# Packing the fetched choices of 32 tokens into full tiles

## The chip, the core and the metric

The kernel runs on one core of one Trainium2 chip. The metric is the device time of one execution in microseconds. Three runs before the change took 2815.97, 2822.40 and 2823.87 us, a median of 2822.4. The engines are TensorE (PE), VectorE (DVE), ScalarE (ACT), GpSimd (POOL) and SyncE (SP), which issues most DMAs; POOL issues the indirect ones. Each engine takes its instructions in the order of its own queue.

## The reference

Two transformer layers run over 256 tokens of 2048 features. The change lies in the second half of the first layer, a product-key mixture of experts with 16,384 experts and 128 choices for each token (8 heads, 16 each):

```
idx, g = top-k over pairs of sub-keys          # 256 tokens x 128 choices
a = einsum('cd,ced->ce', xc, expert_u[ic])     # one dot product per choice
w = g * gelu(a)
y = einsum('ce,ced->cd', w, expert_v[ic])      # weighted sum of 128 rows of v
```

An expert's number is 128 times its first key plus its second. The attention before and the second layer behind are not touched.

## The kernel before

All activations against u are computed densely: 128 streams of two 512 KB loads each, every load split into a high and a low fp32r part (h by ACT, l by DVE, `hi_lo`), then 24 matmuls with 256 columns on PE. Three raw buffers and three split buffers let SP, ACT and DVE run ahead of PE.

For v the experts are parted by their second key. Those from 72 (`PICKED`) on, 56 of 128, are done densely: `build` and `apply` scatter the gates into `grid`, and `dense_rows` streams v twice (two halves of the columns, d = 0 and 1), 56 steps each. Those below 72 are fetched: for every token an indirect DMA on POOL reads up to 128 rows of 8 KB of `v_rows` (`fetch_row`), those of the other sort being out of bounds and left out; another reads the 128 activations (`fetch_act`) from `picked`, a DRAM copy of the gelu outputs. `weigh` multiplies them by the gates into a window of zeros, and four matmuls of 128x32 on 128x512 add the token's row to a bank that holds 32 tokens by 2048 columns.

`choose` finds the choices in the background of the u streams (i from 0 to 52): top-k on DVE, one-hots on POOL and DVE, then for each half of the tokens three transposes of keys and gates on PE, and from them `slots`, `gate`, `at_row` and `at_act`. From i = 75 on, `unit` is called once for every u load and every dense step; at `PACE` 1.27 tokens a call it runs three tokens (`LOT`) at a time. `FETCH` 6 row buffers are in flight, values are fetched 20 tokens ahead (`AHEAD`) and weighed eight at a time (`SOON`). Finished banks are stored to `y_rows` (SP) and read back by POOL (`add_y`), which DVE adds to h. The fetches, the products and the top-k carry order tokens; everything else is ordered by a scheduler by readiness, so the queues differ from the program's order.

Of the kernel before, what the change touches and what calls it, by code (L numbers as in the profile page):

```python
# [26 lines left out]
T = 256  # L27
NM = 16
TM = T + NM
PICKED = 72  # L30
GRID = 128 - PICKED

# [12 lines left out]
def _constants():  # L45
    i = np.arange(128)
    ident = np.eye(128)
    iota = np.broadcast_to(i[None, :], (128, 128))
    base = np.concatenate([ident, iota, np.ones((128, 128))], 1)
    tri = np.where(i[None, :] <= i[:, None], 0.0, NEG)  # L50
    anti = np.where(i[None, :] > i[:, None], 0.0, NEG)
    causal = np.concatenate([tri, np.zeros((128, 128)), tri], 1)
    inv = 10000.0 ** (-(np.arange(32, dtype=np.float32)) / np.float32(32.0))
    inv = np.broadcast_to(inv.astype(np.float32)[None], (128, 32))
    lo = np.tile(_t5_thresholds(), 4)[:, None]
    front = np.concatenate([causal, anti, inv, lo], 1)
# [3 lines left out]
    return [np.ascontiguousarray(a.astype(np.float32)) for a in (base, front, back)]  # L60

# [22 lines left out]


def _layout(a):
    base, front, back = _constants()
    x = a["x"][0]  # L90
    L = {"c_base": base, "c_front": front, "c_back": back}
    L["x"] = x.reshape(2, 128, D)
    L["xT"] = x.T.reshape(KD, 128, T).transpose(1, 0, 2)
    pos = a["positions"][0]
# [207 lines left out]
def bc(ap, shape):  # L302
    return ap.to_broadcast(shape)
# [14 lines left out]
def chain(*gens):  # L318
    for g in gens:
        yield from g  # L320
# [571 lines left out]
def experts(S, I, x2, r2, started, keep, bst, grid, alloc_xn, close_x2, close_xn, late, picked, y_rows):  # L892
# [34 lines left out]
    sc_ = carve(2, 16, 128)  # L927
    keysT = carve(16, 128)
    bcr = carve(T)
    spare = [carve(T) for _ in range(4)]  # L930
    S.load(keysT, I["keysT"])

    def renorm(k):

# [36 lines left out]
    gate = rp.tile([128, T], F32, name="gate")  # L971
    at_row = rp.tile([128, T], U32, name="at_row")
    at_act = rp.tile([128, T], U32, name="at_act")
    got = rp.tile([128, T], F32, name="got")
    fetched = [rp.tile([128, D], F32, name=f"fetched{i}") for i in range(FETCH)]

    windows = [rp.tile([128, 33, 32], F32, name=f"window{i}") for i in range(2)]

    def choose():
        iota16 = S.iota[:, 0:16]  # L980
        for t in range(2):
# [41 lines left out]
            ve.tensor_copy(gate[:, ts], ps[:, 256:384])  # L1023

            x, y = eqs[0].rearrange("p a b -> p (a b)")[:, :128], eqs[1].rearrange("p a b -> p (a b)")[:, :128]
            po.tensor_scalar(x, slots[:, 1, ts], PICKED - 0.5, 128.0 * PICKED, ALU.is_ge, ALU.mult)
            po.tensor_tensor(x, x, slots[:, 1, ts], op=ALU.add)
            ve.scalar_tensor_tensor(x, slots[:, 0, ts], float(PICKED), x, ALU.mult, ALU.add)
            ve.tensor_copy(at_row[:, ts], x)
            ve.scalar_tensor_tensor(y, x, float(T), S.iota, ALU.mult, ALU.add)  # L1030
            if t:
                po.tensor_scalar(y, y, 128.0, None, ALU.add)
            ve.tensor_copy(at_act[:, ts], y)
            yield

    made = {}
# [31 lines left out]

    acts = picked.rearrange("i j (t o) -> (i j t) o", o=1)

    def fetch(*args, **kw):
        tc.stamp_issue_order_token(po.indirect_dma_start(*args, **kw).ins, 'po')  # L1072

    def fetch_act(t):
        fetch(got[:, t:t + 1], None, acts, bass.IndirectOffsetOnAxis(at_act[:, t:t + 1], 0),
                              bounds_check=128 * PICKED * T - 1, oob_is_err=False)

    def fetch_row(t):
        fetch(fetched[t % FETCH], None, I["v_rows"], bass.IndirectOffsetOnAxis(at_row[:, t:t + 1], 0),
                              bounds_check=128 * PICKED - 1, oob_is_err=False)  # L1080

    def weigh(t0):

        ve.tensor_tensor(windows[t0 // 32 % 2][:, t0 % 32:t0 % 32 + 8, 31], got[:, t0:t0 + 8], gate[:, t0:t0 + 8], op=ALU.mult)

    def picks():

        for t in range(AHEAD):
            fetch_act(t)
        for t in range(0, SOON, 8):  # L1090
            weigh(t)
        yield
        stages = []
        for t in range(T):
            g, tt = t // 32, t % 32
            if tt == 0:
                out = S.bank()
            w = windows[g % 2].rearrange("p a b -> p (a b)")[:, 32 * tt + 31 - tt:32 * tt + 63 - tt]
            r = fetched[t % FETCH]
            for c in range(4):  # L1100
                S.mm(out[32 * c:32 * c + 32], w, r[:, 512 * c:512 * c + 512], start=tt == 0, stop=tt == 31)
            if t + FETCH < T:
                fetch_row(t + FETCH)
            if t + AHEAD < T:
                fetch_act(t + AHEAD)
            if t % 8 == 2 and t + SOON < T + 2:
                weigh(t + SOON - 2)
            if tt == 31:
                stage = rw.tile([128, 512], F32, tag="stage", name=S.name("stage"))
                act.copy(stage, out)  # L1110
                stages.append((t + 2, g, stage))
            if stages and (t >= stages[0][0] or t == T - 1):
                _, g_, stage = stages.pop(0)
                for c in range(4):
                    S.load(y_rows[32 * g_:32 * g_ + 32, 512 * c:512 * c + 512], stage[32 * c:32 * c + 32])
            yield
# [16 lines left out]
    for i in range(128):  # L1133
        S.pe_token = 'pe' if i >= PICKED else None
        for a in S.stationary_steps(I["u"], 2 * i, 2, 8, 128, xn, slice(0, T)):
            if i >= PICKED + LEADP:
                unit()
        if i < PICKED:
            if i % 4 == 0:
                lot = rw.tile([128, 4, T], F32, tag="lot", name=S.name("lot"))  # L1140
            act.activation(lot[:, i % 4], a, AF.Gelu_apprx_tanh)
            if i % 4 == 1 and pending:
                S.load(*pending.pop())
            if i % 4 == 3:
# [12 lines left out]
        due += CR  # L1157
        if due >= 1.0:
            next(bg, None)
            due -= 1.0  # L1160
        if i == FIRST - 2:
            for _ in bg:
                pass
            S.token = None
            for f in fetched + windows + [got]:
                po.memset(f, 0.0)
            for t in range(FETCH):
                fetch_row(t)
            build(0)
            ahead = 4  # L1170
        while ahead and gated < T and gated < (i + 2 - FIRST) * RATE:
            if ahead < T:
                build(ahead)
                ahead += 4
            apply(gated, max(i + 1 - PICKED, 0))
            gated += 4
    while gated < T:
        if ahead < T:
            build(ahead)
            ahead += 4  # L1180
        apply(gated, GRID)
        gated += 4
    ob.close()
    close_xn()

# [8 lines left out]
    def add_y(t, c):  # L1194
# [3 lines left out]
        ve.tensor_tensor(h[:, t, cs], h[:, t, cs], y, op=ALU.add)  # L1198

    for d, i in dense_rows(S, wp, I["v"], GRID, lambda i: grid[:, i], evac):  # L1200
# [12 lines left out]
    return h  # L1213
# [457 lines left out]
```

## Time and profile before

| | |
|---|---|
| median of three runs | 2822.4 us |
| profiled execution | 2810.0 us |
| its span, first to last instruction | 2808.2 us |
| PE busy | 2741.8 us (98%) |
| DVE, ACT, POOL busy | 1604.4, 1337.8, 724.4 us |
| granted clock of PE, mean | 0.993 |

Busy time of PE is a union: matmuls overlap in it, so the step from one to the next is read from their starts. A group's mean is the duration of one instruction; a DVE or POOL row's bracket gives the idle time before it and what ended it. The DMA share is the mean busy share of the core's 16 DMA engines.

### The profile page before, as it was taken

The page shows a single profiled execution, that of the slowest core. Times are in us where ns is not written, and L with a number is a line of the kernel's source. Part 1 is how long each engine was busy: PE and PEld are TensorE (multiplying, and loading weights), DVE is VectorE, ACT ScalarE, POOL GpSimd, SP SyncE. Part 2 cuts the span into 40 slices and gives each one's busy share as a digit, 9 for nine tenths or more (in the row PEclk, how much of TensorE's full clock was granted, in tenths as well). Part 3 has the DMA queues.
Part 4 walks back from the last instruction along what each step waited for, and adds up shares of the span by engine and source line. Part 5 has one row for each costly group of instructions (what it writes and reads, how often), then busy time and mean ns, then how long its engine had stood idle before and what let it go on. Part 6 is the DMA issues. An engine that isn't in the chain of part 4 may idle for free.

```text
span 2808.2 us, 48986 instructions
## 1 busy us (share of the span) xinstructions
PE 2741.8 (98%) x19080; PEld 2325.8 (83%) x19080; DVE 1604.4 (57%) x2652; ACT 1337.8 (48%) x2306; POOL 724.4 (26%) x675
## 2 busy tenths in 40 slices
PE   7999999999998999999999999999999999999998
PEld 5977999999996777777566666898789999988886
DVE  5867788677664555543344445654654444466665
ACT  5654544444553444432333334543445555555554
POOL 1200003202016666665767761102000000000000
PEclk9999999999999999999999999999999999999999
DMA  6533656766666888898989997544656666666665
GB/s 209 152 131 114 209 173 199 262 218 222 205 189 214 289 299 301 293 323 297 323 321 340 343 323 246 165 155 125 188 180 194 195 193 193 194 194 195 188 194 165
DMA packets 177064, 625.81 MB, mean 223 GB/s; under 512 B 41321, under 2 KB 42217, under 8 KB 156665
## 3 DMA queue, kind: packets, MB, share of 16 engines
q1 hardware_dynamic: 131200, 462.64, 52.0%
q0 software_dynamic: 45632, 160.05, 15.7%
q8 instruction: 149, 2.44, 0.3%
q14 instruction: 83, 0.68, 0.1%
HBM read 717.52 MB, written 15.73 MB: 261 GB/s over the span
## 4 chain that ended last, share of the span: by engine, by line
PE 90%; DMA 3%; DVE 2%; issue 2%; ACT 2%; POOL 0%; SPq 0%; DVEq 0%; POOLq 0%; ACTq 0%
PE bank L188 84%; PE bank L289 1%; DVE l L194 1%; PE bank L1057 1%; ACT h L193 1%; DMA r<-u 1%; DMA xT<-xT 0%; ACT dump L495 0%; DMA r<-w_k 0%; DMA r<-w_in_a 0%; DMA y<-y_rows 0%; DMA r<-w_in_b 0%; DMA mt<-meta 0%; PE bank L1419 0%; PE bank L703 0%
## 5 line engine op out<-in xcount | busy, mean ns | idle before, releaser
L194 DVE TENSOR_TENSOR l<-r,h 128x1024 fp32r<-128x1024 f32 (+3 forms) x838 | 1023.7, 1225 | 731.6 <-ACT h L193 636.7
L193 ACT ACTIVATE h<-r 128x1024 fp32r<-128x1024 f32 (+3 forms) x838 | 878.3, 1049 | 892.6 <-PE bank L188 644.6
L188 PE MATMUL bank<-xnh,l 128*128 128x256 f32 x2048 | 571.4, 279 | 15.5 <-DVE l L194 9.8
L188 PE MATMUL bank<-xnh,h 128*128 128x256 f32 x2048 | 578.0, 282 | 4.2 <-issue 2.8
L188 PE MATMUL bank<-xnl,h 128*128 128x256 f32 x2048 | 570.4, 279 | 2.3 <-issue 2.2
L188 PE MATMUL bank<-h,w 128*128 128x512 f32 x1920 | 530.9, 394 | 7.1 <-ACT w L193 3.9
L188 PEld LDWEIGHTS bank<-h,w 128*128 128x128 f32 x1920 | 358.2, 189 | 117.2 <-issue 35.8
L188 PEld LDWEIGHTS bank<-xnh,h 128*128 128x128 f32 x2048 | 388.4, 190 | 34.1 <-issue 22.2
L188 PEld LDWEIGHTS bank<-xnh,l 128*128 128x128 f32 x2048 | 388.3, 190 | 16.4 <-DVE l L194 10.8
L188 PEld LDWEIGHTS bank<-xnl,h 128*128 128x128 f32 x2048 | 388.7, 190 | 3.1 <-issue 3.1
L1072 POOL DMA_INDIRECT fetched<-v_rows,at_row x256 | 303.7, 1186 | 212.8 <-PE bank L188 153.2
L1072 POOL DMA_INDIRECT got<-picked,at_act x256 | 283.7, 1108 | 200.6 <-DMA r<-u 119.8
L188 PE MATMUL bank<-l,w 128*128 128x512 f32 x960 | 298.8, 392 | 0.9 <-DVE l L194 0.9
L188 PE MATMUL bank<-zh,h 128*128 128x256 f32 x1024 | 282.7, 276 | 0.0
L188 PE MATMUL bank<-zh,l 128*128 128x256 f32 x1024 | 282.6, 276 | 0.0
L188 PE MATMUL bank<-zl,h 128*128 128x256 f32 x1024 | 282.6, 276 | 0.0
L188 PE MATMUL bank<-fetched,window 128*32 128x512 f32 x2048 | 245.6, 598 | 1.3 <-issue 1.0
L188 PEld LDWEIGHTS bank<-l,w 128*128 128x128 f32 x960 | 181.1, 189 | 40.0 <-DVE l L194 1.3
L188 PEld LDWEIGHTS bank<-zl,h 128*128 128x128 f32 x1024 | 192.2, 188 | 0.0
L188 PEld LDWEIGHTS bank<-zh,h 128*128 128x128 f32 x1024 | 192.2, 188 | 0.0
L188 PEld LDWEIGHTS bank<-zh,l 128*128 128x128 f32 x1024 | 192.2, 188 | 0.0
L1550 POOL TENSOR_TENSOR h2t<-h2t,fw 128x512 f32<-128x512 f32 x4 | 6.4, 1634 | 641.0 <-ACT jk L1548 641.0
(414 smaller groups left out, 3588.4 us busy)
## 6 DMA issues: line engine op xcount, KB each, us to landing
r<-u SPq DMA_DIRECT2D x256, 512.0 KB
r<-w SPq DMA_DIRECT2D x256, 512.0 KB
r<-v SPq DMA_DIRECT2D x112, 512.0 KB
r<-w_out SPq DMA_DIRECT2D x64, 512.0 KB
r<-wq SPq DMA_DIRECT2D x32, 512.0 KB
r<-w_in_c SPq DMA_DIRECT2D x24, 384.0 KB
picked<-lot SPq DMA_DIRECT2D x18, 512.0 KB
r<-w_v SPq DMA_DIRECT2D x16, 512.0 KB
```

Source lines behind the costliest of these rows:

```text
L188: i = self.nc.tensor.matmul(*args, **kw)
L193: self.nc.scalar.activation(hi, src, AF.Copy)
L194: self.order(self.nc.vector.tensor_tensor(lo, src, hi.bitcast(F32), op=ALU.subtract))
L289: self.nc.tensor.transpose(out, src, self.ident[:p, :p])
L1057: pe.matmul(bank[:, tt * 2 * GRID:(tt + 1) * 2 * GRID], oh[:, tt], gv[:, tt].rearrange("p s i -> p (s i)"), start=True, stop=True)
L1072: tc.stamp_issue_order_token(po.indirect_dma_start(*args, **kw).ins, 'po')
L1550: po.tensor_tensor(hs, hs, fw[:, cs_], op=ALU.mult)
```

## The change

The choices below 72 of 32 tokens (`GROUP`) are numbered in order and packed into tiles of 128. A group gets 21 tiles (`PACKS`), so 168 tiles take the place of 256 tokens. `choose` counts each choice's place: a mask, two fp32 matmuls with triangular constants (`c_pick`) for the count of earlier choices, and from the sum a tile number and a row (`place`). `pack` then moves six facts of each choice (first key, second key, token in the group, gate in three bf16 parts) to that place with bf16 one-hot matmuls, four tokens a step: `here` (row) and `mine` (tile) on DVE, `what` on POOL, four matmuls; behind the eighth step of a group it computes the addresses. The 64 steps are called at i = 20 to 51 and at every second i from 55. `multiply` builds 32 columns of weights for a tile from its tokens and gates on DVE. Group totals decide at run time, for two groups at a time, whether `beyond` does what doesn't fit into 21 tiles; the four branches stand at d = 1, i = 40, and all four reads of y behind them, where two stood at i = 4 and 8. `PACE` is 0.84, `AHEAD` 12, `SOON` 4.

```diff
+    before = (i[:, None] < i[None, :]).astype(np.float64)
+    pick = np.concatenate([before, before * (i[:, None] // GROUP == i[None, :] // GROUP), i[:, None] // GROUP == i[None, :4]], 1)
...
-AHEAD, SOON = 20, 8
+AHEAD, SOON = 12, 4
 LASTY = 40
 LOT = 3
-LEADP, PACE = 3, 1.27
+ARM = 2
+LEADP, PACE = 3, 0.84
...
+            fa = facts[:, :, ts]
+            po.tensor_scalar(fa[:, 0], slots[:, 0, ts], -128.0, None, ALU.add)
+            po.tensor_copy(fa[:, 1], slots[:, 1, ts])
+            x, y, z = (eqs[j].rearrange("p a b -> p (a b)")[:, :128] for j in range(3))
+            yu = y.bitcast(U32)
+            ve.tensor_copy(yu, S.iota)
+            ve.tensor_scalar(yu, yu, GROUP - 1, None, ALU.bitwise_and)
+            po.tensor_copy(fa[:, 2], yu)
+            part = z.bitcast(BF16)[:, :128]
+            ve.tensor_copy(part, ps[:, 256:384])
+            ve.tensor_copy(fa[:, 3], part)
+            ve.tensor_tensor(x, ps[:, 256:384], fa[:, 3], op=ALU.subtract)
+            ve.tensor_copy(part, x)
+            ve.tensor_copy(fa[:, 4], part)
+            ve.tensor_tensor(fa[:, 5], x, fa[:, 4], op=ALU.subtract)
+
+            n = es[:, 0:1]
+            po.tensor_scalar(x, ii[:, 1], PICKED - 0.5, None, ALU.is_lt)
+            ve.tensor_reduce(n, x, axis=AX, op=ALU.add)
+            ve.tensor_scalar(y, S.ones, n, None, ALU.mult)
+            po.tensor_scalar(x, slots[:, 1, ts], PICKED - 0.5, None, ALU.is_lt)
+            ps = S.bank()
+            pe.matmul(ps[:, 0:128], pk[:, 0:128], x, start=True, stop=False)
+            pe.matmul(ps[:, 0:128], y, pk[:, 128:256], start=False, stop=True)
+            pe.matmul(ps[:, 128:132], y, pk[:, 256:260], start=True, stop=True)
+            act.copy(total[:, 4 * t:4 * t + 4], ps[:, 128:132])
+            po.tensor_scalar(x, x, -8192.0, 8192.0, ALU.mult, ALU.add)
+            ve.tensor_tensor(x, x, ps[:, 0:128], op=ALU.add)
+            zu = z.bitcast(U32)
+            ve.tensor_copy(zu, x)
+            ve.tensor_scalar(yu, zu, 7, None, ALU.logical_shift_right)
+            ve.tensor_scalar(zu, zu, 127, None, ALU.bitwise_and)
+            po.tensor_copy(place[:, 0, ts], yu)
+            po.tensor_copy(place[:, 1, ts], zu)
...
+    def pack(g, first, n, c0):
+
+        bank = S.bank()
+        for t0 in range(GROUP * g, GROUP * g + GROUP, 4):
+            of = lambda a, m: bc(a[:, t0:t0 + 4][:, :, None], [128, 4, m])
+            here = rw.tile([128, 4, 128], BF16, tag="here", name=S.name("here"))
+            mine = rw.tile([128, 4, n], F32, tag="mine", bufs=1, name=S.name("mine"))
+            what = rw.tile([128, 4, 6, n], BF16, tag="what", name=S.name("what"))
+            ve.tensor_tensor(here, bc(S.iota[:, None, :], [128, 4, 128]), of(place[:, 1], 128), op=ALU.is_equal)
+            ve.tensor_tensor(mine, bc(S.iota[:, None, first:first + n], [128, 4, n]), of(place[:, 0], n), op=ALU.is_equal)
+            for tt in range(4):
+                po.tensor_tensor(what[:, tt], bc(mine[:, tt][:, None, :], [128, 6, n]), bc(facts[:, :, t0 + tt][:, :, None], [128, 6, n]), op=ALU.mult)
+            for tt in range(4):
+                t = t0 % GROUP + tt
+                pe.matmul(bank[:, :6 * n], here[:, tt], what[:, tt].rearrange("p f k -> p (f k)"), start=t == 0, stop=t == GROUP - 1)
+            if t0 % GROUP == GROUP - 4:
+                f = bank[:, :6 * n].rearrange("p (f k) -> p f k", k=n)
+                cs = slice(c0, c0 + n)
+                x, y = S.tmp(32, F32, "px")[:, :n], S.tmp(32, F32, "py")[:, :n]
+
+                ve.tensor_scalar(x, f[:, 0], 128.0, float(PICKED), ALU.add, ALU.mult)
+                ve.tensor_tensor(x, x, f[:, 1], op=ALU.add)
+                ve.tensor_copy(at_row[:, cs], x)
+                act.copy(tok[:, cs], f[:, 2])
+                ve.scalar_tensor_tensor(y, x, float(T), tok[:, cs], ALU.mult, ALU.add)
+                ve.tensor_scalar(y, y, float(GROUP * g), None, ALU.add)
+                ve.tensor_copy(at_act[:, cs], y)
+                act.copy(gate[:, cs], f[:, 5])
+                ve.tensor_tensor(gate[:, cs], gate[:, cs], f[:, 4], op=ALU.add)
+                ve.tensor_tensor(gate[:, cs], gate[:, cs], f[:, 3], op=ALU.add)
+            yield
...
+    def weigh(n, m=1):
+        ve.tensor_tensor(gate[:, n:n + m], gate[:, n:n + m], got[:, n:n + m], op=ALU.mult)
+
+    def multiply(out, n, rows, first, last):
+
+        w = rw.tile([128, GROUP], F32, tag="w", bufs=6, name=S.name("w"))
+        ve.tensor_scalar(w, S.iota[:, 0:GROUP], tok[:, n:n + 1], gate[:, n:n + 1], ALU.is_equal, ALU.mult)
+        for c in range(4):
+            S.mm(out[GROUP * c:GROUP * c + GROUP], w, rows[:, 512 * c:512 * c + 512], start=first, stop=last)
...
+            multiply(out, n, fetched[n % FETCH], k == 0, k == PACKS - 1)
+            if n + FETCH < NP:
+                fetch_row(n + FETCH, fetched[n % FETCH])
+            if n + AHEAD < NP:
+                fetch_act(n + AHEAD)
+            if n % SOON == 1 and n + SOON - 1 < NP:
+                weigh(n + SOON - 1, min(SOON, NP - n - SOON + 1))
...
+    def beyond(groups):
+
+        more = 4096 // 128 - PACKS
+        for g in groups:
+            for _ in pack(g, PACKS, more, 0):
+                pass
+            out = S.bank()
+            for n in range(more):
+                fetch_act(n)
+                fetch_row(n, fetched[n % FETCH])
+                weigh(n)
+                multiply(out, n, fetched[n % FETCH], n == 0, n == more - 1)
...
+    packing = chain(*[pack(g, 0, PACKS, PACKS * g) for g in range(8)])
...
+        if FIRST - 34 <= i < FIRST - 2 or i >= FIRST and i % 2:
+            next(packing, None)
...
+    ve.tensor_reduce(most, total.rearrange("p (a b) -> p a b", b=ARM), axis=AX, op=ALU.max)
+    ve.tensor_copy(most_i, most)
...
-        if d == 1 and i in (4, 8):
-            add_y(0, i // 8)
-        if d == 1 and i in (LASTY + 1, LASTY + 2):
-            add_y(1, i - LASTY - 1)
+        if d == 1 and i == LASTY:
+            for a in range(8 // ARM):
+                n = nc.values_load(most_i[0:1, a:a + 1], min_val=0, max_val=4096)
+                with tc.If(n > 128 * PACKS):
+                    beyond(range(ARM * a, ARM * a + ARM))
+        if d == 1 and LASTY < i <= LASTY + 4:
+            add_y(h, (i - LASTY - 1) // 2, (i - LASTY - 1) % 2)
```

PE's queue at the transposes of the first half of the tokens, before. `xnh` and `h_`/`l_` are the normalised tokens and the parts of u, `gridt` the scratch of `choose`:

```order
L188 MATMUL bank_5687<-xnh,l_5720 128x256
L289 MATMUL bank_5755<-base,gridt 128x128 x3
L188 MATMUL bank_5770<-xnh,h_5772 128x256 [waits Activation_49]
L188 MATMUL bank_5770<-xnl,h_5772 128x256
L188 MATMUL bank_5770<-xnh,l_5773 128x256 [waits DVE_49]
```

and now:

```order
L192 MATMUL bank_5690<-xnh,l_5723 128x256
L293 MATMUL bank_5758<-base,gridt 128x128 x3
L1056 MATMUL bank_5781<-gridt 128x128 [waits Pool_49]
L1057 MATMUL bank_5781<-gridt 128x128 [waits DVE_49]
L1058 MATMUL bank_5781<-gridt 128x4
L192 MATMUL bank_5793<-xnh,h_5795 128x256 [waits Activation_49]
```

The three prefix matmuls (L1056 to L1058) stand between the transposes and the next u matmuls, the first waiting for POOL, the second for DVE.

DVE's queue behind these transposes now, its last twelve instructions up to the reduce that the prefix sum needs (`oh`, `ec` and `gv` belong to `build`, `l` to a u stream):

```order
L198 TENSOR_TENSOR l_5858<-r_5856,h_5857 128x1024 [waits DMAHW4_49]
L1044 CAST facts<-gridt 128x128 [waits DVE_49]
L1080 TENSOR_TENSOR ec_8694<-base,slots 128x224
L1045 TENSOR_TENSOR gridt<-bank_5758,facts 128x128 [waits DVE_49]
L1081 TENSOR_TENSOR gv_8695<-ec_8694,slots 128x4x56 [waits DVE_49]
L1046 CAST gridt<-gridt 128x128 [waits DVE_49]
L1079 TENSOR_TENSOR oh_8766<-base,slots 128x512
L1047 CAST facts<-gridt 128x128 [waits DVE_49]
L1080 TENSOR_TENSOR ec_8767<-base,slots 128x224
L1048 TENSOR_TENSOR facts<-gridt,facts 128x128 [waits DVE_49]
L1080 TENSOR_TENSOR ec_8846<-base,slots 128x224 [waits Activation_49]
L1052 TENSOR_REDUCE gridt<-gridt 128x1 [waits Pool_49]
```

Of what stands before the reduce (L1052), the l and the one-hots belong to other work; the reduce itself waits for POOL.

PE's queue at the first branch now, behind the products of the dense step i = 40 (`most_i` holds the groups' totals):

```order
L192 MATMUL bank_18196<-l_19453,w_19457 128x512
L192 MATMUL bank_18195<-h_19452,w_19458 128x512
L192 MATMUL bank_18196<-h_19452,w_19458 128x512
L1314 TENSOR_LOAD most_i [waits DVE_49]
L1315 COMPARE_AND_BRANCH
L1119 LDWEIGHTS here_19489 [waits DVE_49]
```

What follows the compare is the body for a group that is too full; it is jumped over when the group fits, and the next branch stands behind it.

## Rows read from the trace of the kernel before

**Rows 1.** The page's busy times: engine, us, share, instructions; and its chain shares.
```profile
PE 2741.8 (98%) x19080; PEld 2325.8 (83%) x19080; DVE 1604.4 (57%) x2652; ACT 1337.8 (48%) x2306; POOL 724.4 (26%) x675
...
PE 90%; DMA 3%; DVE 2%; issue 2%; ACT 2%; POOL 0%; SPq 0%; DVEq 0%; POOLq 0%; ACTq 0%
```

**Rows 2.** Windows: length, busy us by engine (instructions), granted clock, DMA share, GB/s.
```profile
660.00:680.00 20.00, 20.00 (x179) 20.00 (x178) 15.46 (x25) 8.52 (x11) 7.47 (x8) 1.00 0.75 235
840.00:860.00 20.00, 11.76 (x72) 11.36 (x72) 7.35 (x16) 3.79 (x10) 15.74 (x15) 0.81 0.24 60
866.00:1300.00 434.00, 422.56 (x3501) 322.63 (x3500) 219.88 (x407) 178.87 (x435) 284.68 (x247) 0.99 0.85 295
866.00:1723.00 857.00, 838.35 (x5848) 587.30 (x5851) 392.21 (x632) 330.72 (x648) 557.50 (x489) 0.99 0.88 310
1348.00:1723.00 375.00, 371.63 (x2047) 233.32 (x2051) 158.59 (x206) 137.87 (x195) 243.41 (x215) 0.99 0.91 324
1500.00:1600.00 100.00, 100.00 (x563) 63.17 (x565) 46.21 (x60) 39.16 (x55) 73.24 (x65) 1.00 0.96 343
```

**Rows 3.** Timeline of PE while v streams: start, us, line, operation, count.
```profile
1700.41 0.73 PE L188 MATMUL bank<-h,w 128*128 128x512 f32 x2
...
1708.81 0.73 PE L188 MATMUL bank<-h,w 128*128 128x512 f32 x2
...
1717.21 0.72 PE L188 MATMUL bank<-h,w 128*128 128x512 f32 x2
...
1722.89 1.07 PE L188 MATMUL bank<-fetched,window 128*32 128x512 f32 x8
```

**Rows 4.** The page's DMA queues: packets, MB, share of 16 engines.
```profile
q0 software_dynamic: 45632, 160.05, 15.7%
```

**Rows 5.** Timeline of PE at 103 us: the bf16 matmuls and what follows.
```profile
103.02 0.87 PE L650 MATMUL bank<-dTb,oh 128*128 128x64 bf16 x24
103.73 0.48 PE L188 MATMUL bank<-h,kvhl 128*128 128x512 f32 x1
```

**Rows 6.** Chain that ended last: start us, us, what.
```profile
719.60 0.39 PE bank L1057 x4
...
743.58 5.51 PE bank L188 x48
...
850.87 1.00 POOL got L1072
852.17 2.77 DMA got<-picked,at_act
```

**Rows 7.** Timeline of DVE behind the second half's transposes.
```profile
710.55 0.28 DVE L1022 TENSOR_TENSOR slots<-bank,gridt 128x128 f32<-128x128 f32 x1
710.75 0.27 DVE L1023 COPY gate<-bank 128x128 f32<-128x128 f32 x1
```

**Rows 8.** Groups of POOL: names, shapes, count | busy us, mean ns | idle before.
```profile
L1003 POOL TENSOR_TENSOR gridt<-gridt,base 128x256 f32<-128x256 f32 x32 | 26.3, 831 | 33.8 <-DVE gridt L1005 32.7
...
L1026 POOL TENSOR_SCALAR gridt<-slots 128x128 f32<-128x128 f32 x2 | 1.8, 908 | 48.0 <-DVE slots L1018 48.0
...
L1027 POOL TENSOR_TENSOR gridt<-gridt,slots 128x128 f32<-128x128 f32 x2 | 1.4, 705 | 0.2
```

**Rows 9.** Timeline of DVE at the start of the fetching, waits in brackets.
```profile
844.84 0.17 DVE L1084 TENSOR_TENSOR window<-got,gate 128x8 f32<-128x8 f32 x1 [9.44 <-DMA got<-picked,at_act]
...
846.11 0.39 DVE L1047 TENSOR_TENSOR gv<-ec,slots 128x224 fp32r<-128x224 f32 x1
846.41 0.68 DVE L1045 TENSOR_TENSOR oh<-base,slots 128x512 fp32r<-128x512 f32 x1
...
856.25 0.17 DVE L1084 TENSOR_TENSOR window<-got,gate 128x8 f32<-128x8 f32 x1 [7.78 <-DMA got<-picked,at_act]
```

**Rows 10.** Timeline of PE after a gap at 1290 us.
```profile
1291.39 0.42 PE L188 MATMUL bank<-xnl,h 128*128 128x256 f32 x1
1291.61 0.41 PE L188 MATMUL bank<-xnh,l 128*128 128x256 f32 x1
```

More of the change, by code (lines that the diff above doesn't have):

```diff
@@ L31 @@
 GRID = 128 - PICKED
+GROUP = 32
+PACKS = 21
 def _t5_thresholds():
@@ L88, in _layout @@
 def _layout(a):
-    base, front, back = _constants()
+    base, front, back, pick = _constants()
     x = a["x"][0]
-    L = {"c_base": base, "c_front": front, "c_back": back}
+    L = {"c_base": base, "c_front": front, "c_back": back, "c_pick": pick}
     L["x"] = x.reshape(2, 128, D)
@@ L929, in experts @@
     bcr = carve(T)
+    pk = carve(260)
     spare = [carve(T) for _ in range(4)]
     S.load(keysT, I["keysT"])
+    S.load(pk, I["c_pick"])
     def renorm(k):
@@ L969, in experts @@
     slots = ow.tile([128, 4, T], F32, bufs=1, name="slots")
[L971 to L974, printed above, removed]
+    facts = rp.tile([128, 6, T], F32, name="facts")
+    place = rp.tile([128, 2, T], F32, name="place")
+    total = rp.tile([128, 8], F32, name="total")
+    NP = 8 * PACKS
+    at_row = rp.tile([128, NP], U32, name="at_row")
+    at_act = rp.tile([128, NP], U32, name="at_act")
+    tok = rp.tile([128, NP], F32, name="tok")
+    gate = rp.tile([128, NP], F32, name="gate")
+    got = rp.tile([128, NP], F32, name="got")
     fetched = [rp.tile([128, D], F32, name=f"fetched{i}") for i in range(FETCH)]
-    windows = [rp.tile([128, 33, 32], F32, name=f"window{i}") for i in range(2)]
     def choose():
@@ new lines, in weigh, with store @@
+    def weigh(n, m=1):
[5 more added lines that the diff above has]
+            S.mm(out[GROUP * c:GROUP * c + GROUP], w, rows[:, 512 * c:512 * c + 512], start=first, stop=last)
+    def store(to, g, out, wait=None):
+        stage = rw.tile([128, 512], F32, tag="stage", name=S.name("stage"))
+        act.copy(stage, out)
+        yield
+        for c in range(4):
+            S.load(to[GROUP * g:GROUP * g + GROUP, 512 * c:512 * c + 512], stage[GROUP * c:GROUP * c + GROUP])
@@ L1086, in picks @@
     def picks():
[L1088 to L1091, printed above, removed]
+        for n in range(AHEAD):
+            fetch_act(n)
+        weigh(0, SOON)
         yield
[L1093 to L1096, printed above, removed]
+        stores = []
+        for n in range(NP):
+            g, k = n // PACKS, n % PACKS
+            if k == 0:
                 out = S.bank()
-            w = windows[g % 2].rearrange("p a b -> p (a b)")[:, 32 * tt + 31 - tt:32 * tt + 63 - tt]
-            r = fetched[t % FETCH]
-            for c in range(4):
[L1101 to L1116, printed above, removed]
@@ new lines, in picks @@
+            multiply(out, n, fetched[n % FETCH], k == 0, k == PACKS - 1)
[5 more added lines that the diff above has]
+                weigh(n + SOON - 1, min(SOON, NP - n - SOON + 1))
+            if k == PACKS - 1:
+                stores.append((n + 2, store(y_rows, g, out)))
+                next(stores[-1][1])
+            if stores and (n >= stores[0][0] or n == NP - 1):
+                next(stores.pop(0)[1], None)
@@ new lines, in picks @@
+            yield
+    def beyond(groups):
[5 more added lines that the diff above has]
+            for n in range(more):
+                fetch_act(n)
+                fetch_row(n, fetched[n % FETCH])
+                weigh(n)
+                multiply(out, n, fetched[n % FETCH], n == 0, n == more - 1)
+            stage = rw.tile([128, 512], F32, tag="stage", name=S.name("stage"))
+            for c in range(4):
+                S.load(stage[GROUP * c:GROUP * c + GROUP], y_rows[GROUP * g:GROUP * g + GROUP, 512 * c:512 * c + 512])
+            ve.tensor_tensor(stage, stage, out, op=ALU.add)
+            for c in range(4):
+                S.load(y_rows[GROUP * g:GROUP * g + GROUP, 512 * c:512 * c + 512], stage[GROUP * c:GROUP * c + GROUP])
@@ L1164, in experts @@
             S.token = None
-            for f in fetched + windows + [got]:
+            for f in fetched + [got]:
                 po.memset(f, 0.0)
-            for t in range(FETCH):
-                fetch_row(t)
+            for n in range(FETCH):
+                fetch_row(n, fetched[n])
             build(0)
@@ L1182, in experts @@
         gated += 4
+    for _ in packing:
+        pass
     ob.close()
```

35 lines of the change are left out of this document (14 added, 21 removed).

## Prediction

> **What bounds the kernel now.** I read the page's busy shares and chain first, then the windows by stage, then the timelines around the work that changes. PE is busy for 2741.8 of 2808.2 us and holds 90% of the chain that ends last [rows 1], so time on PE's queue is nearly time of the kernel. The windows show a second limit beside it. While choices are fetched, from 866 to 1723 us, PE is busy for 838 of 857 us, but the DMA engines are busy too: 0.85 in the part that streams u (866 to 1300), 0.91 in the part that streams v (1348 to 1723), and 0.96 with 343 GB/s in the fullest 100 us [rows 2]. The reader is to see both: PE time that goes is worth its full price only until the DMA engines are full. In the stage before the fetching PE is always busy, and DVE is busy for 15.5 of 20 us [rows 2], so DVE has little to spare there.
>
> **The products removed.** The v timeline gives the price of one fetched tile: from 1700.41 to 1708.81 us (8.40) PE runs 24 matmuls of two dense steps and three tokens, from 1717.21 to 1722.89 (5.68) the 24 matmuls alone [rows 3]. Three tokens cost 2.72 us, one 0.91; the eight matmuls of the single token at the end last 1.07. 256 tokens become 168 packs, 88 fewer: 88 x 0.91 = **80 us off PE** (94 at 1.07). The products keep their shape (four of 128x32 on 128x512), and DVE builds their weights off PE's path. On POOL 512 indirect issues become 336; POOL was not late before. The bytes stay: the page's software queue moved 160.05 MB [rows 4], and less 2.1 MB of y this is 157.9 MB or some 19,280 rows of 8 KB, which is what 168 packs must carry too (150.6 full ones, the rest part empty). That is 2,410 rows for a group of 32 tokens; a group has room for 2,688, and counting the reference's own choices gives at most 2,463. So the code beyond the room is stepped over, and its price is that of the branches.
>
> **The packing added on PE.** 64 steps of four bf16 matmuls of 126 columns. The nearest rows: 24 bf16 matmuls of 64 columns take 0.71 us, from 103.02 to 103.73 [rows 5], 30 ns each, so 126 columns some 58 ns and a step 0.23 us; four fp32r matmuls of 112 columns take 0.39 us in the chain [rows 6]. I take 0.30, nearer to the bf16 row: 64 x 0.30 = **+19 us** (15 to 25). 32 steps and ten more come before the fetching, 22 beside it.
>
> **The prefix sums: a new wait on PE's queue.** In choose(), three more fp32 matmuls stand right behind the three transposes, twice, with no u matmul between. Today u matmuls follow at once, and DVE and POOL do their part beside them. Now PE holds u's matmuls behind a chain: slots copied on DVE, facts, the count, a mask on POOL, and only then the matmul. On DVE the timeline shows a pitch of 0.2 us for 128-column operations [rows 7] and, elsewhere, 0.3 for a gv and 0.68, the last tenth of it covered, for a one-hot [rows 9]. For the first half of the tokens DVE's queue from the copy to the reduce holds the copy (0.4), an l (1.2), two one-hots, three ec (0.3 each), a gv and eight short ones, about 5.6 us; POOL's mask adds 0.9 [rows 8] and the hand-overs 0.5: some 7.0 us, and the prefix matmuls 0.5 of their own. For the second half there are no one-hots: some 5.9 us with the matmuls, in the same way. Together 13.4, **+14 us** with the drain before them (1 if DVE and POOL had all inputs early; 18 with every operation at its full duration). Nothing covers it: u's matmuls sit behind it on the same queue.
>
> **DVE behind it.** After the prefix matmul DVE runs four short operations, waits for two POOL casts (0.75 each, as POOL's 128-column rows [rows 8]), builds mine and here (0.2 and 0.7 [rows 7, 9]), and then, since mine has one buffer, waits twice for four POOL multiplies before it gets to the next l. With 0.7 us a multiply (128 columns on POOL cost 0.7 to 0.9 [rows 8]) the l comes some 11 us after PE resumed, and PE has three streams of 2.76 us in stock (24 matmuls, half of a chain piece of 5.51 us [rows 6]), 8.3 us. Twice 2.6 us plus the lumps of top-k behind it: **+7 us** (0 to 14).
>
> **The four branches.** No row of before shows a branch or a register read from SBUF. From below, a queue event costs nothing one could see (0.1 us each); from above, each costs two trips to memory of 2.77 us, the time the chain shows for the smallest fetch, issue included [rows 6]: 0.4 to 22 us. I take one trip without POOL's 1.00 us of issue in front of it [rows 6], 1.8 us each: **+7 us**. PE meets them with both queues before it run ahead: five v loads stand in front of SP's branch, so SP's wait there for all its loads is covered. SP's own four register reads stand earlier, among the u loads behind the second prefix chain: four trips of 1.8 us are 7, inside the 8.3 us that PE has in stock and beside the 11 us that DVE takes there, so 0.
>
> The Trainium skill ("Runtime: NRT & Kernel Launch", Instruction fetch mechanics) speaks against this part: a taken branch that leaves the fetched window stalls until its page has come. The jumped code is 172 instructions on PE and under 100 elsewhere, less than the 256 of a block there, so by that rule the jumps would mostly be free; the page's 1.3 us for a register load would make four 5 us. No run here shows it yet.
>
> **PE's clock after a stall.** Rows after 1291 us show u matmuls every 0.22 us after such a gap [rows 10] where the chain has 5.51 us for 48, 0.115 each [rows 6]: some 23 of them cost 2.3 us more. In the window 840 to 860 the granted clock was 0.81 of the 2.4 GHz [rows 2]. Three such stalls: **+7 us** (0 to 10).
>
> **DMA in the fetch stretch.** Packs are full for 18 of 21, so the same rows come in fewer steps. In the u part 106 units carried 134 tokens and will carry 89 packs: PE gives back 45 x 0.91 less 22 x 0.30, 34 of 434 us, and the DMA share rises from 0.85 to 0.92: nearly free, I take 3 us. In the v part 122 tokens become 79 packs: 39 of 375 us, and the share would rise from 0.91 to 1.02 [rows 2], which cannot be. At 0.97, the fullest row plus a little, the part takes 352 us, 16 more than PE wants. Together **+18 us** (0 if the share can reach 1; 52 if the mean stays at 0.90).
>
> **The start of the fetching.** Today DVE waits 9.4 and 7.8 us for fetched values [rows 9], and PE is busy for only 11.8 of 20 us [rows 2]. 12 instead of 20 are fetched ahead, and the first weighing needs four, not eight: **-7 us** (-10 to 0).
>
> The y loads move behind the branches: DVE adds four instead of two there, 5 us beside 43 us of v matmuls, with the streams in stock: 0.
>
> **Sum.** -80 + 19 + 14 + 7 + 7 + 7 + 18 - 7 = **-15 us**. The profiled execution took 2810.0 us (1.8 around its span), 12 us under the median of 2822.4 of the runs shown; on the median the change gives 2807 us.
>
> **Rivals.**
> - *The waits are hidden.* DVE and POOL keep far enough ahead, the DMA engines take the load, and only the packing and the branches remain: -80 + 19 + 7 - 7 = -61, **2761 us**. For it: before the fetching PE is busy for 20.00 of 20 us although DVE is at 15.5 [rows 2]. Against it: the prefix matmul is behind its producers in the order itself.
> - *The DMA engines become the bound (slower).* The place is the fetch stretch, 857 us at 0.88 on average. If the share can only rise to s, the stretch saves 857 x (1 - 0.88/s) and not 73 us: at 0.90 19 to 21 us. With 13 for the early packing, 14 + 7 + 7 + 7 for the waits and -7 this is +20, **2842 us**. It decides from a share under 0.924, where the saving no longer pays for the 41 us. For it: bursts, 18 full packs and then three near-empty ones, with six buffers. Against it: 0.96 was held for 100 us with PE at 100% [rows 2].
> - *POOL paces the packing.* If a multiply with two broadcast operands costs 1.5 us, twice the 0.7 of the row with 128 columns, four take 6.0 us and with POOL's own 1.7 a step (two of 0.83 [rows 8]) make 7.7 us against PE's 6.2: 32 steps x 1.5 = 48 more, **2855 us**. It decides from about 1.1 us a multiply. For it: the broadcast rows of 256 columns cost more than the plain ones of 128 [rows 8]. Against it: 126 columns are half of 256.
>
> **How the numbers follow.** The forecast (2792 to 2822) has 0.50, hidden waits 0.22, DMA 0.17, POOL 0.11. A measurement here can tell 0.3%, 8.5 us. Faster by more than that: 0.31 of the first, 0.21 of the second, 0.03 of the third, 0.55. Within: 0.15 + 0.06, 0.21. Slower: 0.24. The range 2765 to 2845 leaves a tenth on either side.
>
> **What would show it.** Right: fetched matmuls 1344 instead of 2048 at the same length; PE gaps of 5 to 8 us at two L1056 matmuls, released by POOL; four short gaps at L1315; a DMA share near 0.95 from the first fetch to the last. Wrong: u matmuls following the transposes without a gap; a DMA share still near 0.88; a PE gap of 15 us or more at the branches, or any instruction of beyond() executed.

## The result and the profile after

The changed kernel took 2803.6 us (2795.6 to 2805.9, six runs), the kernel before, run beside it, 2821.5 (2816.0 to 2825.4): a ratio of 0.9935 (0.9918 to 0.9953), 18 us less, where 15 were forecast. That is not the end of it. When both ran again for the experiments, the changed kernel took 2798.9 us and the kernel before 2780.0: 1.0065 (1.0052 to 1.0078), slower. Both differences lie outside their intervals and are under 1%. The changed kernel is nearly the same on both occasions, the kernel before is not, and a term that the prediction does not have, 36 us, stands in both.

The page of the changed kernel, busy times in us; PE has 22 us less than in [rows 1]:

```profile
PE 2719.8 (97%) x18644; PEld 2367.7 (85%) x18644; DVE 1710.9 (61%) x3042; ACT 1339.9 (48%) x2324; POOL 680.7 (24%) x764
```

Its windows, in the columns of [rows 2]: u's part of the fetching, v's part, and the fullest 100 us. The DMA share is 0.89, 0.94 and 0.97, and PE stays busy all the same:

```profile
922.00:1322.00 400.00, 397.37 (x3368) 334.95 (x3365) 262.06 (x561) 182.65 (x445) 249.99 (x249) 1.00 0.89 333
1322.00:1673.00 351.00, 345.64 (x1790) 229.89 (x1792) 175.89 (x293) 143.55 (x200) 170.83 (x147) 1.00 0.94 361
1500.00:1600.00 100.00, 100.00 (x522) 66.50 (x521) 54.06 (x91) 40.35 (x56) 53.40 (x47) 1.00 0.97 374
```

PE's waits in total (us, times, longest), of the changed kernel and then of the kernel before:

```profile
PE bank L192 <- PEq L1315: 16.2, 1, 16.2
PE bank L192 <- DVE l L198: 14.0, 19, 3.4
PE bank L1056 <- POOL gridt L1054: 13.0, 2, 7.0
```

```profile
PE bank L188 <- DVE l L194: 15.8, 15, 5.3
PE bank L188 <- issue: 14.5, 26, 2.0
```

The two gaps at the prefix sums are there, released by POOL, 7.0 and 6.0 us long. The largest wait is the branches, 16.2 us in one piece. The waits for l, the part that DVE makes of each stream, are no longer than before.

The timeline of PE at the last fetched packs and the branches answers to [rows 3]: three packs still take 2.72 us (1671.21 to 1673.93). The bracket is the idle time before an instruction.

```profile
1671.21 2.78 PE L192 MATMUL bank<-fetched,w 128*32 128x512 f32 x24
1673.93 0.73 PE L192 MATMUL bank<-h,w 128*128 128x512 f32 x2
...
1696.00 1.19 PE L192 MATMUL bank<-h,w 128*128 128x512 f32 x2 [16.20 <-PEq L1315]
```

And at a packing step: the four matmuls take 0.21 us, and the u matmul behind them another 0.21 to the next start instead of 0.12:

```profile
660.01 0.28 PE L192 MATMUL bank<-xnh,l 128*128 128x256 f32 x1
660.13 0.40 PE L1119 MATMUL bank<-what,here 128*128 128x126 bf16 x4
660.34 0.36 PE L192 MATMUL bank<-xnh,h 128*128 128x256 f32 x1
660.55 0.27 PE L192 MATMUL bank<-xnl,h 128*128 128x256 f32 x1
660.66 0.28 PE L192 MATMUL bank<-xnh,l 128*128 128x256 f32 x1
```

What the prediction did not look for shows in matmuls that the change does not touch. Two windows of stretches with nothing but u's and zh's matmuls of 256 columns, 60 and 200 us long, where PE never stops; the number behind PE's busy time is the count of matmuls. First the kernel before, then the changed one:

```profile
440.00:500.00 60.00, 60.00 (x532) 60.00 (x531) 46.75 (x86) 29.07 (x37) 14.25 (x17) 1.00 0.67 214
2150.00:2350.00 200.00, 200.00 (x1767) 200.00 (x1766) 90.53 (x74) 102.84 (x147) 0.00 (x0) 1.00 0.64 195
```

```profile
440.00:500.00 60.00, 60.00 (x508) 60.00 (x507) 45.66 (x89) 27.75 (x34) 15.57 (x18) 1.00 0.66 206
2150.00:2350.00 200.00, 200.00 (x1688) 200.00 (x1687) 86.46 (x71) 98.61 (x141) 0.00 (x0) 1.00 0.61 186
```

In 60 us 532 matmuls became 508, in 200 us 1767 became 1688: from 113 ns to 118 between two starts. The granted clock is 1.00 in all four rows. u has 6144 such matmuls and zh 3072.

The stages by the starts of matmuls (us): until the first of u, from there to the last of u, from there to the first of zh (it holds v and the branches), and from there to the last of all.

| | to u | u | v | zh and rest |
|---|---|---|---|---|
| before, first trace | 420.2 | 904.9 | 773.7 | 698.2 |
| before, second trace | 418.6 | 882.0 | 771.0 | 698.2 |
| after, first trace | 420.5 | 901.9 | 751.1 | 714.5 |
| after, second trace | 419.9 | 901.2 | 752.3 | 714.6 |

The last stage holds nothing of the change and is 16.3 us longer.

### The profile page after: what moved, and what is told of

It reads as the page before. It is cut to its first block, busy times and chain, and to the rows that moved or that the text cites. A ratio compares the mean times of both kernels' runs of the same rounds, so it can differ in the third digit from the quotient of the medians.

```text
span 2799.3 us, 48568 instructions
## 1 busy us (share of the span) xinstructions
PE 2719.8 (97%) x18644; PEld 2367.7 (85%) x18644; DVE 1710.9 (61%) x3042; ACT 1339.9 (48%) x2324; POOL 680.7 (24%) x764
## 5 line engine op out<-in xcount | busy, mean ns | idle before, releaser
L192 PE MATMUL bank<-xnh,l 128*128 128x256 f32 x2048 | 581.3, 284 | 9.3 <-DVE l L198 8.1
L192 PE MATMUL bank<-xnh,h 128*128 128x256 f32 x2048 | 589.3, 288 | 0.0
L192 PE MATMUL bank<-xnl,h 128*128 128x256 f32 x2048 | 580.5, 283 | 1.4 <-issue 1.1
L192 PE MATMUL bank<-h,w 128*128 128x512 f32 x1920 | 530.5, 395 | 20.1 <-PEq L1315 16.2
L192 PE MATMUL bank<-zh,l 128*128 128x256 f32 x1024 | 288.2, 281 | 0.0
L1140 POOL DMA_INDIRECT fetched<-v_rows,at_row x168 | 202.9, 1208 | 248.1 <-PE bank L192 214.3
L1140 POOL DMA_INDIRECT got<-picked,at_act x168 | 194.7, 1159 | 55.4 <-issue 49.4
L1116 POOL TENSOR_TENSOR what<-mine,facts 128x126 bf16<-128x126 f32 x256 | 137.3, 566 | 196.8 <-PE bank L1119 168.3
```

The source lines that it names most:

```text
L192: i = self.nc.tensor.matmul(*args, **kw)
L1116: po.tensor_tensor(what[:, tt], bc(mine[:, tt][:, None, :], [128, 6, n]), bc(facts[:, :, t0 + tt][:, :, None], [128, 6, n]), op=ALU.mult)
L1140: i = po.indirect_dma_start(*args, **kw)
```

## Experiments

The first four (both pads of 64 bytes, the one without branches, the one with the prefix sums put off) ran on chip 0 beside a kernel before of 2807.6 us. The other eight ran on chip 8: four beside 2780.0 us and the last four beside 2780.5. The chip of the first measurement is not on record. Since the kernel before moves, the ratios are given, but stages are compared between traces. Two kernels are the unchanged two, for a base.

**The place of the stream parts.** The change adds two small constants (`most`, `most_i`) to the first pool, 64 bytes a partition with padding. Every tile behind them on the left side of SBUF then stands 64 bytes further, h and l of the streams too; xn and z, on the right, do not move.

```diff
+        S.const.tile([128, 16], F32, name="pad")
         warm = S.const.tile([128, 1], F32, name="warm")
```

> The changed kernel with an unused tile of 64 bytes a partition in the first pool, which moves every tile on the left side of SBUF (the halves h and l of the streams among them) by 64 bytes and changes no instruction. Theory A (the address): in the kernel after, the u matmuls follow each other every 0.119 us, before every 0.113, and those of zh every 0.119 against 0.113; the new constants moved h and l from 32 to 96 modulo 128 bytes, where xn and z stand too. With the pad h and l are at 32 again: pitch back to 0.113 in both stages, 6144 x 0.006 + 3072 x 0.0055 = 50 us less, 2754 us. Rival B (the pitch comes from the instruction stream, which now holds branches, or from the packing beside it): pitch stays at 0.119, 2804 us.

> The kernel before with the same 64-byte pad and nothing of the change. Theory A: h and l move from 32 to 96 modulo 128, where xn and z stand: pitch of the u and zh matmuls 0.119 instead of 0.113, 50 us more, 2872 us. Rival B: there is no branch and no packing, pitch stays 0.113, 2821 us.

The kernel before with the pad: 2837.4 us, a ratio of 1.0116 (1.0097 to 1.0136). It has no packing and no branch, and its zh stage now has the pace of the changed kernel:

```profile
2150.00:2350.00 200.00, 200.00 (x1687) 200.00 (x1687) 85.82 (x71) 98.97 (x141) 0.00 (x0) 1.00 0.62 185
```

That ends rival B. The changed kernel with the pad took 2795.7 us, 0.9965 (0.9953 to 0.9977), and its pace is a third one, not that of before:

```profile
2150.00:2350.00 200.00, 200.00 (x1700) 200.00 (x1700) 87.04 (x71) 99.09 (x141) 0.00 (x0) 1.00 0.62 187
```

So theory A is wrong with modulus 128. The addresses in the four built programs suggest 256: the distance from the moving tile (xn, z) up to the weights (h, l) is 64 in the kernel before, 128 in the changed one and in the padded one before, 192 in the padded one after. The next two try that, the second by moving xn alone.

```diff
+        S.const.tile([128, 48], F32, name="pad")
...
+        if name == "xn":
+            p.tile([128, 48], F32, name="pad")
```

> The changed kernel with an unused tile of 192 bytes a partition in the first pool instead of 64. Theory A, mended: what counts is the distance between the weights' and the moving tile's addresses modulo 256. So far 64 went with 113.3 ns, 128 with 119, 192 with 118, 0 (x2) with 120. With 192 more, h and l are at 32 modulo 256 and the distance to xn and z is 64 again: 113.3 ns in both stages, 9216 x 5.4 ns = 50 us less than the changed kernel, or 30 if only as much comes back as the pad cost the kernel before. Rival (the distance doesn't decide, the 113 ns belong to something else in the kernel before): 118 to 120 ns and the time of the changed kernel.

> The changed kernel with 192 unused bytes above xn, which moves xn alone (from 224 to 32 modulo 256) and leaves h, l and z. If the distance decides: u matmuls every 113.3 ns, those of zh still 119, 6144 x 5.4 ns = 33 us less than the changed kernel, some 20 if part is lost to waits. If the place of h and l itself decides (32 modulo 256): no change, 119 ns in both.

With the pad of 192 bytes the changed kernel took 2763.4 us, a ratio of 0.9942 (0.9927 to 0.9956), 35.5 us under the changed kernel beside it. Both stretches have the counts of the kernel before:

```profile
440.00:500.00 60.00, 60.00 (x532) 60.00 (x531) 46.02 (x85) 29.59 (x37) 14.23 (x17) 1.00 0.68 217
2150.00:2350.00 200.00, 200.00 (x1767) 200.00 (x1766) 90.04 (x74) 103.83 (x148) 0.00 (x0) 1.00 0.65 194
```

With xn moved it took 2778.3 us, 0.9993 (0.9984 to 1.0002), 20.6 us under the changed kernel. In one run u has the short pace and zh the long one, as the distances say:

```profile
440.00:500.00 60.00, 60.00 (x531) 60.00 (x531) 47.32 (x90) 29.11 (x36) 14.78 (x18) 1.00 0.67 214
2150.00:2350.00 200.00, 200.00 (x1687) 200.00 (x1687) 86.18 (x71) 98.99 (x143) 0.00 (x0) 1.00 0.60 185
```

The distance decides, not the place of h by itself (96 modulo 256 here, as in the changed kernel).

> The changed kernel itself, as the base for the kernels beside it. u and zh matmuls every 119 ns, as in its first trace; a ratio to the kernel before of 0.9935 as measured (0.9918 to 0.9953), and 2790 us if this chip runs the kernel before in 2808 us, as with the last four kernels. If instead the gain depends on the chip, a ratio nearer 1: no_branch (2785) and prefix_later (2793) would then stand 16 and 8 us under some 2801 us.

> The kernel before itself, for a trace of it beside the others. If the pitch belongs to the layout of SBUF: 113.3 ns between u matmuls and between those of zh, as in its first trace. If it belongs to the chip or to the single run: 118 to 119 ns, as all other kernels show so far.

The changed kernel took 2798.9 us, the kernel before 2780.0, so the gain does depend on the occasion. Whether that is the chip is open: the kernel before took 2807.6 us on chip 0, and 2780.0 and 2780.5 on chip 8, and no run holds everything but the chip fixed. The kernel before kept its pace in zh (1767 matmuls in 200 us), which settles that the pace is the program's. Where it lost time in the first trace is the u stage, 904.9 us against 882.0. PE's waits in the second trace:

```profile
PE bank L188 <- DVE l L194: 14.9, 14, 4.3
...
PE bank L188 <- issue: 1.3, 1, 1.3
```

"Issue" is 1.3 us instead of 14.5, and 10.6 of the 14.5 lie between 880 and 1290 us, while u streams and rows are fetched. The weight loads of the first trace there show what it looks like:

```profile
1031.37 0.19 PEld L188 LDWEIGHTS bank<-xnl,h 128*128 128x128 f32 x1 [0.55 <-issue]
1032.07 0.19 PEld L188 LDWEIGHTS bank<-xnh,l 128*128 128x128 f32 x1 [0.51 <-issue]
1032.78 0.19 PEld L188 LDWEIGHTS bank<-xnh,h 128*128 128x128 f32 x1 [0.53 <-issue]
```

PE waits for no other engine here and gets one weight load every 0.7 us instead of every 0.11. Between 880 and 1290 us the second trace has no such place. What held the instructions back was not found, and the rest of the 22.9 us between the two u stages is not accounted for.

**The branches.** The experiment drops lines 1313 to 1316 and leaves the totals in place.

> The changed kernel without the four branches and the code behind them (which does nothing for these inputs); totals are still reduced. If the one PE gap of 16.2 us at the branches is their whole price: 2804 - 16 = 2788 us, and up to 3 us less for the clock behind it. Rival (the sum's 7 us, the rest of the gap being a wait that something else would then show): 2797 us. Theory A on the pitch: u matmuls still every 0.119 us. Rival B, if the branches slow the instruction stream: 0.113.

It took 2784.6 us, 0.9932 (0.9910 to 0.9953). The v stage is 733.3 us instead of 751.1: 17.8 us, the gap and a little more. No wait stands at the branches' place any more; one of 4.2 us for `w`, 340 us ahead of it, stands in this trace alone. The instructions at the branches in the changed kernel, with shortest, median and longest duration in ns:

```profile
L1315 PEldq COMPARE_BRANCH  x4: 3615/4537/5124, 1676.1 to 1690.7; - x4
L1315 SPq COMPARE_BRANCH  x4: 45/45/53, 1679.8 to 1686.6; - x4
```

```profile
L1314 SPq TENSOR_LOAD <-most_i x4: 262/272/467, 751.4 to 753.4; - x4
...
L1314 PEldq TENSOR_LOAD <-most_i x4: 304/312/495, 1675.5 to 1690.3; - x4
```

The compare takes SP 45 ns and PE 3.6 to 5.1 us. What the prediction feared, the load of the total, is 0.3 us. The first of PE's four compares ends at 1679.7 us, while matmuls issued before it still run (to 1679.8), so the gap of 16.2 us holds three jumps, 5.4 us each with their loads.

The prediction counted 172 PE instructions in the code that is jumped over, and under 100 elsewhere. The built program has 239 in each body, 152 of them matmuls, and over 100 on DVE and POOL too. The Trainium skill ("Runtime: NRT & Kernel Launch", Instruction fetch mechanics) has a taken branch stall when its target lies outside the fetched window. The prediction took from it that these jumps would mostly be free; they were not, and whether they left that window no run shows. The 1.3 us that the prediction had for a register load was 0.3 here.

The next kernel has the 192-byte pad too.

```diff
-ARM = 2
+ARM = 1
```

> The changed kernel with the 192-byte pad and a branch for every group, eight instead of four, each over half the code (78 rows of PE between two compares instead of 153). If a branch has a price of its own, some 4.4 us: PE gap of 35 us at the compares and 18 us more than with the pad alone, 2781 us. If the price goes with the code that is jumped over: 18 us as with four, 2763 us.

It took 2773.1 us, 0.9968 (0.9953 to 0.9983). The compares up to 1652.9 us, those behind, and the one wait behind them all:

```profile
L1315 PEldq COMPARE_BRANCH  x2: 369/401/433, 1647.7 to 1652.0; - x2
```

```profile
L1315 PEldq COMPARE_BRANCH  x6: 2637/3157/4897, 1653.0 to 1673.6; - x6
```

```profile
PE bank L192 <- PEq L1315: 25.0, 1, 25.0
```

25.0 us lie between the two expectations. With the pad and four branches the gap is 17.3 us:

```profile
PE bank L192 <- PEq L1315: 17.3, 1, 17.3
```

In both kernels the first jump runs beside matmuls but for at most 0.3 us. So three jumps over 152 matmuls hold 17.3 us, 5.8 each, and seven over 76 hold 25.0, 3.6 each: less code makes a jump cheaper, but half the code does not make it half the price. Length is not all of it, since two of the eight jumps took 0.4 us and the other six 2.6 to 4.9 over bodies of the same length. What sets the difference is not shown.

**The prefix sums.**

```diff
             po.tensor_scalar(x, slots[:, 1, ts], PICKED - 0.5, None, ALU.is_lt)
+            yield
             ps = S.bank()
             pe.matmul(ps[:, 0:128], pk[:, 0:128], x, start=True, stop=False)
```

> The changed kernel with the prefix sums of each half put off by one step of choose(), two u loads later (96 PE rows), so that u matmuls stand between the transposes and them. If PE's two gaps of 7.0 and 6.0 us at L1056 are paid in full: both go, 2804 - 13 = 2791 us, and the l waits behind them (the DVE term, up to 7 us) shrink as well. Rival (the time is lost anyway, because DVE and POOL are late with u's parts): 2804 us and PE waits for l and h grow by as much as L1056 loses.

It took 2793.4 us, 0.9955 (0.9939 to 0.9971). The u stage is 889.9 us instead of 901.9. One of the two gaps is gone; for the second half the scheduler still put the three matmuls right behind the transposes, and its gap is left:

```profile
PE bank L1057 <- POOL gridt L1054: 5.7, 1, 5.7
```

So the 7.0 us of the first half were paid in full here; by the stage, 5 us more went with them, 2.6 of them waits for l (11.4 us against 14.0).

**The DMA engines.** A halved bound in `fetch_row` leaves out half of the rows and no product (in `before_half` in the kernel before).

```diff
-              bounds_check=128 * PICKED - 1, oob_is_err=False)
+              bounds_check=64 * PICKED - 1, oob_is_err=False)
```

> The changed kernel with the 192-byte pad; rows of v from the middle on are out of bounds and left out, so that about half of the 158 MB is fetched, with every product still made. If the DMA engines hold PE in the fetch stretch as the sum had it (18 us): the stretch from the last u matmul to the first of zh, 751.8 us with the pad, gets 16 us shorter, u's part 2 to 3. If PE sets the pace there although the DMA share is 0.95 to 0.97: under 5 us in both.

> The kernel before with half the rows fetched in the same way. In its first trace u's part took 904.9 us, in its second 882.0, with the same pitch of 113.3 ns where nothing is fetched. If the fetched bytes are what makes u's part long on some occasions, u's part takes 882 us or less here wherever it runs, and the kernel gains on the full kernel before by as much as that one stands above 2780 us; if not, no change.

The changed kernel with half the rows took 2746.9 us, 0.9878 (0.9862 to 0.9895), against 2763.4 for the same kernel with all rows: 16.5 us. Windows from the first packs on, u and v, with half the rows and with all:

```profile
922.00:1291.00 369.00, 369.00 (x3224) 310.13 (x3224) 253.37 (x537) 174.66 (x425) 244.77 (x238) 1.00 0.76 250
1292.00:1635.00 343.00, 343.00 (x1778) 229.86 (x1781) 178.81 (x292) 145.10 (x199) 171.47 (x147) 1.00 0.78 262
```

```profile
922.00:1299.00 377.00, 373.23 (x3251) 312.48 (x3244) 254.54 (x542) 174.19 (x427) 241.23 (x239) 1.00 0.91 342
1299.00:1650.00 351.00, 345.40 (x1788) 229.60 (x1790) 175.31 (x293) 143.69 (x199) 173.15 (x147) 1.00 0.94 360
```

With half the rows the DMA share is 0.76 and 0.78 and PE has no gap. The stages are 8.0 and 6.3 us shorter: in v between the two expectations, in u more than either. The kernel before gained 6 us, 0.9977 (0.9964 to 0.9989), its stages 7.9 and 4.9. Since its full version stood at 2780.5 us on that occasion, this does not tell whether the fetched bytes made u's part long in the first trace. So fetching costs PE something in both kernels; by the times the changed one pays 10 us more, by the two pairs of traces 2.

**Together.** The pad of 192, the `yield`, and x2 moved by 192 bytes as well.

> The changed kernel with the 192-byte pad, the prefix sums of the first half put off (of the two gaps only the first went when this was tried alone), and 192 unused bytes ahead of x2, which bring the distance between h and x2 from 0 to 64 modulo 256. From the kernel with the pad (2763 us beside a kernel before of 2780): 7 us for the gap of the first half and some 2 of waits behind it; if the distance decides a third time, x2 matmuls every 113.3 ns instead of 120, 768 x 6.7 ns = 5 us. Together 2749 us, a ratio of 0.989 on a chip that runs the kernel before in 2780 us. If distance 64 is nothing special, x2 stays at 120 and 2754 us.

It took 2753.3 us, a ratio of 0.9897 (0.9879 to 0.9915): faster than both kernels, by 27 us against the kernel before and, over two sets with the same kernel before, 46 against the changed one. From the kernel with the pad it is 10 us, not the 14 expected: in its one trace, of the slowest of its five runs, u's stage is only 1.9 us shorter (877.3 against 879.2), though the first gap is gone. x2's matmuls, 256 of the 768 in each row, before and then here, with first and last start: 98.7 us became 94.5, with a median of 276 ns instead of 283.

```profile
L188 PE MATMUL bank<-x2h,h x256: 278/283/365, 319.5 to 418.2; 128*128 128x256 f32 x128
```

```profile
L192 PE MATMUL bank<-x2h,h x256: 276/276/369, 319.7 to 414.2; 128*128 128x256 f32 x128
```

That is the third pair of tiles for which distance 64 gave the short pace.

## Why the prediction came out

The time was right, and the sum of the edits too, but only for a kernel whose tiles stay where they were. With the 192-byte pad the change is worth -16.6 us beside a kernel before of 2780.0, against -15 forecast. The measured -18 is that sum, plus 36 for the moved tiles, minus 37 because the kernel before ran 41.5 us longer on the first occasion and the changed one 4.7 (2821.5 less 2780.0; 2803.6 less 2798.9). Two things that the prediction did not have cancelled, and that they did is luck. The step that failed is not one of its terms but a premise: every matmul that the change does not touch was taken at its old price, 113 ns from start to start, and it was 118 to 119.

By its terms:

- **Products removed, -80.** Right: three packs take 2.72 us, as in [rows 3], and 88 x 0.91 is 80.
- **Packing, +19.** Right: the four matmuls take 0.21 us, close to the 0.23 from the bf16 row [rows 5], and the u matmul behind them loses 0.09 more. From 660.01 to 660.66 us three u starts take 0.65 us instead of 0.36, so a step costs 0.29, and 64 of them 19. The 0.30 was a choice between two rows, and its last 0.07 was not reasoned.
- **Prefix sums, +14.** Right in place and releaser, and nearly in size: 13.0 us of waits and twice 1.3 for the matmuls, 16 in all.
- **DVE behind them, +7.** The waits for l were 15.8 us before and 14.0 after. With the short pace, where PE asks sooner, 20.1 against 14.9 in the second trace of before: 5. The row of the kernel with the pad:

```profile
PE bank L192 <- DVE l L198: 20.1, 22, 3.9
```

- **Branches, +7.** Mis-sized: 16 to 18. It was priced as a trip to memory; the load is cheap and the jump on PE is not. The bound of 22 from above held. It is also the forecast's own mark for wrong, a gap of 15 us or more.
- **PE's clock, +7.** Too high: matmuls that started at 1.2 GHz between 400 and 1800 us cost, from start to start, about 13 us more in the first trace of before and 12 after, in the second traces 10.5 and 14, with the pad 11: 0 to 3.
- **DMA, +18.** Too high: 2 to 10 (and its own parts, 3 and 16, make 19). The share did rise, from 0.91 and 0.96 [rows 2] to 0.94 and 0.97, but a share of 0.97 was no wall: PE was busy for 100.00 of 100 us beside it.
- **Start, -7.** PE's gaps over 1.2 us there add up to 8.2 us in both traces of before and to 6.3 with the pad: -2. All but one of these gaps end with l, so DVE is late with u's parts there as well.
- **Not in the sum: the moved tiles, +36.** 22 us in u and 16 in zh by the traces (901.9 to 879.8 with xn moved, 714.5 to 698.2), 35.5 by the times.

With what each measured, the terms without the moved tiles add up to between -28 and -12; the kernel with the pad showed -16.6.

Of the rivals, the hidden waits did not come: the prefix gaps are there. DMA as a bound did not come either, and the slower outcome of the second occasion, +19, is not its mechanism. POOL did not pace the packing; the multiply's mean is 0.57 us, under the 1.1 from which it would decide, and the median 0.41:

```profile
L1116 POOL TENSOR_TENSOR what<-mine,facts 128x126 bf16<-128x126 f32 x256 | 137.3, 566 | 196.8 <-PE bank L1119 168.3 <-DVE gridt L847 12.1 <-DVE mine L1114 9.4
```

## What to carry to other kernels

A change that adds a few bytes to the first pool moves every tile behind it: compare the start-to-start pace of matmuls that the change does not touch before crediting or blaming the change, and settle it with a pad in the old kernel and one in the new. Price a run-time branch on the engine that is the bound by its jump, not by the load of its condition. And when the base itself moves by more than the effect, compare stages of traces, and measure both kernels on one occasion and one chip.

## What the runs showed of the hardware

- Matmuls of 256 fp32 columns with weights of 128x128 follow each other every 113 to 120 ns, depending on the distance between the two tiles' addresses in a partition. Starts in zh, where nothing else happens, are 113.3 ns apart at distance 64 modulo 256, 118.7 at 128, 117.8 at 192; x2 has a median of 120 at distance 0 and of 113 at 64. All in rows with granted clock 1.00.
- Distance 64 allows the short pace, it does not ensure it: of 256 loads of u (24 matmuls each), 140 ran at 113 ns on the mean in the first trace of before, 115 in the second, 118 with the pad of 192, none in the changed kernel or the padded one before. In most of the others single steps are longer: by the median step, at least 205 of 256 had 113 or 114 ns in each of the three. Why the distance matters, no run shows.
- A compare-and-branch that is taken took PE 3.5 to 6.0 us over 152 matmuls and 0.4 to 4.9 over 76, and the other engines about 0.05; part of it runs beside matmuls issued before. A register load from SBUF takes about 0.3 us on all of them.
- The same program of before differs by 1.5% between occasions (2780 to 2822 us), which may have been on different chips, the changed one by 0.2%. Of the 27 us between the two traces of before 13 are PE waiting for single instructions (14.5 against 1.3 us), most of it while rows were fetched.
